# A two-layer decoder trunk with a top-2-of-8 expert layer on one core: expert 0 with 64 slots in place of 96, three experts gathered together, and the slots' places copied across partitions

## The chip, the cores and the metric

The kernel runs on one core of one Trainium2 chip. The metric is the device time of one execution in microseconds (us). Durations come from one profiled execution of the kernel before.

## The reference

Two residual layers over 256 tokens of 1024 channels, all in float32. Each layer is a mixer (projections, sparse and dilated attention, gates) and a feed-forward part; the first layer's is dense, the second's is a choice of two experts out of eight for each token. Only that last part is touched by the change:

```python
def moe_swiglu(h, router, w1, w3, w2):
    B, S, D = h.shape
    x = h.reshape(B * S, D)
    logits = (x @ router).astype(F32)
    top_v, top_i = lax.top_k(logits, TOP_K)
    wts = jax.nn.softmax(top_v, axis=-1)
    combine = jnp.sum(jax.nn.one_hot(top_i, N_EXPERTS, dtype=F32) * wts[..., None], axis=1)
    out = jnp.zeros((B * S, D), F32)
    for e in range(N_EXPERTS):
        out = out + combine[:, e:e + 1] * swiglu(x, w1[e], w3[e], w2[e]).astype(F32)
    return out.reshape(B, S, D).astype(h.dtype)
```

`w1` and `w3` of an expert are 1024 x 2816, `w2` is 2816 x 1024: 34.6 MB for one expert, 276.8 MB for the eight. After it come a residual add and a final RMSNorm.

## The kernel before, in words

The program runs the first layer (mixer, dense feed-forward), the second layer's mixer, and then the function `moe`. Its stages follow one another on TensorE (PE). Every instruction goes through a helper that records it at one line, L137, so rows are told apart by their tiles.

**Routing and slots.** `moe` ranks the eight logits of each token, and numbers the tokens of each expert: token number n of an expert gets slot n. Experts are taken in an order that depends on how many tokens they have. `PLACE` says which rank stands at which place of the order: rank 0 is always expert 0 (its weights are asked for before the routing is known), and ranks 1 to 7 are the others by falling count. `BLOCKS` says how many blocks of 32 slots the expert at each place has. If some expert has more tokens than slots, `tc.If(ms["over"] > 0)` runs a further pass over all eight experts for the rest. What follows calls an expert by its place, 0 to 7.

**picks and gather.** `picks` makes on VectorE (DVE) a selection matrix `Pm` (token by slot, one where the token has that slot) for a group of `GROUPS`. `gather` multiplies the tokens (`kh`, `kl`, high and low part of each) by it on PE and so brings the group's tokens as columns into the tile `xge`: 8 channel blocks x 2 token halves x 2 parts = 32 matmuls for a group, each as wide as the group's columns. The first gather stands ahead of expert 0; the one of a later group stands inside the last product of the expert before it (`k0 == 12`).

**One expert** of `nb` blocks: `wide_layer` for `w1` and for `w3` (columns up to 2048, 8 weight tiles each), the remaining 768 columns of both (8 tiles, `rest`), then `w2` (11 tiles of two k blocks). A block's 32 slots are the stationary operand, in one of four column strips of 32 of the array. For every weight tile PE goes over the blocks, so an expert with three blocks takes about half as long again on PE as one with two. Behind the second `rest` tile, `places` brings `Pm` into the form `PT` (slot by token), and the transposes `turned` bring the gated activations from `sg` into the tile `He`, which is read by the `w2` products. The scatter (`prev`) multiplies the result by `PT` and adds it to the residual `x`; it stands at the third weight tile of the following expert.

**places before.** `PT` has three variants. They differ in partitions 96 to 127: where an expert has three blocks, the fourth column strip of `w2` holds sums of another block for each third of the columns. For each token half, `places` transposes `Pm` on PE, makes for three blocks two more products of 32 columns with the identity that land on partitions 96 to 127, and copies with ACT and DVE.

**Weights.** 17 tiles of 1 MB hold weights (`rawx`, `raw`, and pairs `whi`, `wlo`). `weight()` issues a load from the SyncE queue (SP) in the order in which the weights are used; a load waits until PE has read the tile that it replaces. The first 17 are issued during the second layer's mixer. For the last expert `w2` is loaded in two column halves, and behind the third tile of the first half the same queue loads the final norm's gain into the tile `xge` (`load_gain`, L310), which must wait until PE has read `xge` for the last time, in the last expert's `rest` products. Every weight load behind it in the queue waits with it.

Of the kernel before, what the change touches and what calls it, by code (L numbers as in the profile page):

```python
# [9 lines left out]
F32 = mybir.dt.float32  # L10
F32R = mybir.dt.float32r
I32 = mybir.dt.int32
AF = mybir.ActivationFunctionType
OP = mybir.AluOpType
AX = mybir.AxisListType

SEQ, D, DEPTH = 256, 1024, 2
HD, ROT = 64, 16
HALF = ROT // 2
NT = SEQ // 128  # L20
DB = D // 128
# [16 lines left out]
SC = HD ** -0.5  # L38


PLACE = 0, 5, 1, 6, 2, 3, 4, 7
BLOCKS = 3, 2, 3, 2, 3, 3, 3, 2

GROUPS = (0,), (1, 2), (3, 4), (5, 6), (7,)

CHUNKS = {2: ((0, 512), (512, 512)), 3: ((0, 352), (352, 336), (688, 336))}
FA = 2048
# [52 lines left out]
def f(ap):  # L100
    return ap.bitcast(F32)
# [3 lines left out]
def tile_hybrid(ctx: ExitStack, tc: tile.TileContext, x, positions, norm_mix, w_in, pos_k, pos_v,  # L105
# [12 lines left out]
    def bank(tag, dt=F32):  # L118
        return psum.tile([128, 512], dt, name="ps_" + tag, tag=tag)
# [26 lines left out]
    V, S, T = Queue("V", nc.vector), Queue("S", nc.scalar), Queue("T", nc.tensor)  # L146

    def mm(o, l, r, start, stop):
        return T.matmul(o, l, r, start=start, stop=stop, skip_group_check=True)

    def tr(o, i, idt):
        return T.transpose(o, i, idt)
# [19 lines left out]
    ident = ct[:, C_ID:C_ID + 128]  # L172
# [273 lines left out]
    def copy(eng, o, i):  # L446
        if eng == "S":
            S.activation(o, i, AF.Copy)
        else:
            V.tensor_copy(o, i)  # L450
# [520 lines left out]
    ms = {}  # L971
# [121 lines left out]
    def moe():  # L1093

        mp, L, kh, kl = ms["mp"], ms["L"], ms["kh"], ms["kl"]
# [22 lines left out]
        rx = mp.tile([128, NT], F32, name="rx")  # L1118
# [10 lines left out]
        slots = ct[:, C_SLOT:C_SLOT + 128]  # L1129
# [37 lines left out]

        def picks(g, sl, blocks):

            Pm = ms["pm"].tile([128, 2, NT, 128], F32R, name="Pm", bufs=2)  # L1170
            for i, r in enumerate(g):
                n = 32 * blocks[r]
                for t in range(NT):
                    for c in range(0, 128, n):
                        m = min(n, 128 - c)
                        V.tensor_tensor(Pm[:, i, t, c:c + m], slots[:, :m], sl[:, t, r:r + 1].to_broadcast([128, m]),
                                        op=OP.is_equal)
            return Pm

        def experts(ep, blocks, bases, Pm=None):  # L1180
            first = bases is None
            if first:
                sl = sls
            else:
                sl = ep.tile([128, NT, NE], F32, name="slot2", bufs=1)
# [2 lines left out]

            def gather(g, Pm, by_tile=False):

                n = 32 * max(blocks[r] for r in g)
                ng = len(g)
                xg = ep.tile([128, DB, 192], F32, name="xge", bufs=1)
                pts = [bank("mm") for _ in range(DB // 2)]
                for ts in ((t,) for t in range(NT)) if by_tile else (range(NT),):
                    for d in range(DB):
                        o = pts[d // 2][:, d % 2 * 256:d % 2 * 256 + ng * n]
                        cs = slice(d * 128, (d + 1) * 128)
                        for t in ts:
                            mm(o, kh[:, t, cs], Pm[:, :ng, t, :n], t == 0 and d % 2 == 0, False)  # L1200
                            mm(o, kl[:, t, cs], Pm[:, :ng, t, :n], False, t == NT - 1)
                for d in range(0, DB, 2):
                    copy("SV"[d // 2 % 2], xg[:, d:d + 2, :ng * n],
                         pts[d // 2].rearrange("p (k c) -> p k c", k=2)[:, :, :ng * n])
                return xg, n

            def scales(Pm):

                rg = ep.tile([128, 16], F32, name="rg", bufs=1)
                pr = bank("a")  # L1210
                for s in range(blocks[0]):
                    for t in range(NT):
                        for c in range(4):
                            mm(pr[32 * c:32 * c + 32, s:s + 1], f(Pm)[:, 0, t, 32 * s:32 * s + 32], rx[:, t:t + 1],
                               t == 0 and s == 0, t == NT - 1)
                V.tensor_copy(rg[:, :blocks[0]], pr[:, :blocks[0]])
                return rg
# [19 lines left out]
            fin = None  # L1237
# [18 lines left out]
                    ms["index"][r] = nc.values_load(ints[0:1, r:r + 1], engines=(mybir.EngineType.SP,),  # L1256
                                                    min_val=0, max_val=NE - 1)

            group = {g[0]: g for g in GROUPS}
            Pms, rg = {}, None  # L1260
            Pms[0] = Pm = Pm or picks(GROUPS[0], sl, blocks)
            in_order("VST" if first else "T")
            xg, wide = gather(GROUPS[0], Pm, by_tile=True)
            if first:
                rg = scales(Pm)
                weights()
# [4 lines left out]
            for r in range(NE):  # L1271
                nb = blocks[r]
                if r in group:
                    g = group[r]
                if r + 1 in group:
                    Pms[r + 1] = picks(group[r + 1], sl, blocks)
                i = g.index(r)
                Pm = Pms[g[0]]
                sc = [rg[:, s:s + 1] if first and r == 0 else None for s in range(nb)]
                He = ep.tile([128, FB, 96], F32, name="He", bufs=1)  # L1280
                xs = [slice(i * wide + 32 * s, i * wide + 32 * s + 32) for s in range(nb)]


                def wide_layer(tag):
# [30 lines left out]
                for k in range(DB):  # L1315
# [5 lines left out]
                    if k == 1:  # L1321
                        PT = places(ep, Pm, i, nb)
# [50 lines left out]
                for half in range(2) if by_half else (None,):  # L1373
                    for k0 in range(0, FB, 4):
                        ks = range(k0, min(k0 + 4, FB))
                        ws = {}
                        if by_half:
                            hs = weight()
                            ws = {k: hs[(k - k0) // 2][:, (k - k0) % 2 * 512:(k - k0) % 2 * 512 + 512] for k in ks}
                        else:  # L1380
                            for k in ks[::2]:
                                ws[k], ws[k + 1] = weight()
                        lanes = [[] for _ in range(4)]
                        for k in ks:
                            for n in range(len(ch)) if half is None else (half,):
                                for s in range(nb):
                                    if nb == 2:
                                        q = k % 2 * 2 + s
                                    else:
                                        q = 3 if s == n and k % 4 != 3 and k < FB - 1 else s  # L1390
                                    lanes[q].append((n, k, s))
                        for j in range(max(len(l_) for l_ in lanes)):
                            for q, l_ in enumerate(lanes):
                                if j < len(l_):
                                    n, k, s = l_[j]
                                    c0, cw = ch[n]
                                    mm(Y[n][32 * q:32 * q + 32, :cw], He[:, k, 32 * s:32 * s + 32],
                                       ws[k] if by_half else ws[k][:, c0:c0 + cw], (q, n) not in marks, k >= FB - 2)
                                    marks.add((q, n))
                        if k0 == 0 and not half:  # L1400
                            for p in range((nb + 1) // 2):
                                turned_rest(p)
                        if k0 == 8 and last and not half:
                            fin = ep.tile([128, DB, 192], F32, name="xge", bufs=1).rearrange("p d c -> p (d c)")
                            load_gain(fin[:, :D], final_norm)
                        if k0 == 12 and r + 1 in group:
                            xg, wide = gather(group[r + 1], Pms[r + 1])
                        if k0 == 4 and half == 1:
                            in_order("VST")
                            final(0)  # L1410
# [17 lines left out]
        def places(ep, Pm, i, nb):  # L1428

            PT = ep.tile([128, 3, SEQ], F32R, name="PT", bufs=1)  # L1430
            pts = [bank(("mm", "a")[t]) for t in range(NT)]
            for t, pt in enumerate(pts):
                tr(pt[:, :128], f(Pm)[:, i, t, :128], ident)
                if nb == 3:
                    for n in (1, 2):
                        mm(pt[96:, n * 128:(n + 1) * 128], f(Pm)[:, i, t, 32 * n:32 * n + 32], ident, True, True)
            for t, pt in enumerate(pts):
                ts = slice(t * 128, (t + 1) * 128)
                S.activation(PT[:, 0, ts], pt[:, :128], AF.Copy)
                if nb == 3:  # L1440
                    V.tensor_copy(PT[:96, 1:, ts], pt[:96, None, :128].to_broadcast([96, 2, 128]))
                    V.tensor_copy(PT[96:, 1:, ts], pt[96:, 128:384].rearrange("p (n c) -> p n c", n=2))
            return PT

        def finish(ep, fin):
# [23 lines left out]
        ms["rk"] = mp  # L1469
        Pm0 = picks(GROUPS[0], slot, BLOCKS)  # L1470
        rstd(rx)
# [67 lines left out]
```

## Time and profile before

| | |
|---|---|
| median of 3 runs | 1320.09 us (1318.83 to 1321.11) |
| the profiled execution's own time | 1320.82 us |
| its span, first to last instruction | 1318.9 us |
| PE busy | 1286.2 us, 98% |
| PE weight loads busy | 855.1 us, 65% |
| DVE busy | 546.9 us, 41% |
| ACT busy | 411.8 us, 31% |
| moved by DMA | 383.32 MB |

How to read it: a busy PE need not be a PE at its peak, since matmuls overlap, and a share over the whole span says nothing about one stage. The experts run from about 631 us to the end. In a row of instructions the first number is the start in us from the span's start, the second the length of the merged run; from the start of one row to the start of the next is what the work of the row costs in time. A float32 matmul shows as two instructions.

### The profile page before, as it was taken

The page shows a single profiled execution, that of the slowest core. Times are in us where ns is not written, and L with a number is a line of the kernel's source. Part 1 is how long each engine was busy: PE and PEld are TensorE (multiplying, and loading weights), DVE is VectorE, ACT ScalarE, POOL GpSimd, SP SyncE. Part 2 cuts the span into 40 slices and gives each one's busy share as a digit, 9 for nine tenths or more (in the row PEclk, how much of TensorE's full clock was granted, in tenths as well). Part 3 has the DMA queues.
Part 4 walks back from the last instruction along what each step waited for, and adds up shares of the span by engine and source line. Part 5 has one row for each costly group of instructions (what it writes and reads, how often), then busy time and mean ns, then how long its engine had stood idle before and what let it go on. Part 6 is the DMA issues. An engine that isn't in the chain of part 4 may idle for free. (4 is left out here: it accounts for less than half of the span.)

```text
span 1318.9 us, 26882 instructions
## 1 busy us (share of the span) xinstructions
PE 1286.2 (98%) x11256; PEld 855.1 (65%) x11256; DVE 546.9 (41%) x1259; ACT 411.8 (31%) x756; POOL 0.2 (0%) x4
## 2 busy tenths in 40 slices
PE   7999999999999999999999999999999999999994
PEld 6888998999888888998337333473335635536431
DVE  6788668666548787676311110201101101110112
ACT  6676546544436576553201010100001001010001
POOL 0000000000000000000000000000000000000000
PEclk9999999999999999998899999999999999999897
DMA  8744435555556654469699999999999999999854
GB/s 289 254 133 124 141 116 192 192 192 192 192 177 200 223 160 118 140 229 417 207 382 399 375 423 419 419 423 418 423 417 414 424 411 422 417 411 424 318 211 190
DMA packets 122945, 383.32 MB, mean 291 GB/s; under 512 B 10720, under 2 KB 17216, under 8 KB 110400
## 3 DMA queue, kind: packets, MB, share of 16 engines
q1 hardware_dynamic: 122816, 381.53, 76.4%
q8 instruction: 90, 1.47, 0.4%
q14 instruction: 39, 0.32, 0.1%
HBM read 380.45 MB, written 1.05 MB: 289 GB/s over the span
## 5 line engine op out<-in xcount | busy, mean ns | idle before, releaser
L137 DVE TENSOR_TENSOR wlo<-raw,whi 128x1024 fp32r<-128x1024 f32 (+1 forms) x186 | 221.8, 1201 | 111.8 <-ACT whi L137 110.7
L137 ACT ACTIVATE whi<-raw 128x1024 fp32r<-128x1024 f32 (+1 forms) x186 | 191.3, 1040 | 160.1 <-PE ps_mm L137 106.0
L137 PE MATMUL ps_mm<-rawx,xge 128*32 128x384 f32 (+1 forms) x1912 | 189.5, 543 | 0.0
L137 PEld LDWEIGHTS ps_mm<-rawx,xge 128*32 128x32 f32 x1912 | 67.9, 111 | 108.8 <-issue 101.4
L137 PE MATMUL ps_mm<-whi,hTh 128*128 128x512 f32 (+2 forms) x320 | 121.2, 379 | 2.4 <-ACT whi L137 2.4
L137 PE MATMUL ps_mm<-hTh,whi 128*128 128x256 f32 x432 | 122.6, 284 | 0.0
L137 PE MATMUL ps_mm<-hTh,wlo 128*128 128x256 f32 x432 | 120.4, 279 | 0.0
L137 PE MATMUL ps_mm<-hTl,whi 128*128 128x256 f32 x432 | 120.4, 279 | 0.0
L137 PE MATMUL ps_mm<-wlo,hTh 128*128 128x512 f32 (+2 forms) x320 | 119.6, 374 | 0.4 <-DVE wlo L137 0.4
L137 PE MATMUL ps_mm<-whi,hTl 128*128 128x512 f32 (+2 forms) x320 | 119.3, 373 | 0.0
L137 PE MATMUL ps_a<-rawx,He 128*32 128x336 f32 (+2 forms) x1104 | 96.4, 493 | 5.6 <-DMA rawx<-in_moe_w_dram 5.6
L137 DVE TENSOR_TENSOR sg<-ps_a,sg 128x512 f32<-128x512 f32 x18 | 12.4, 691 | 186.1 <-PE ps_a L137 186.1
L137 PEld LDWEIGHTS ps_mm<-hTh,whi 128*128 128x128 f32 x432 | 81.7, 189 | 1.7 <-issue 1.0
L137 PEld LDWEIGHTS ps_a<-rawx,He 128*32 128x32 f32 x1104 | 54.6, 112 | 42.9 <-issue 18.0
L137 PEld LDWEIGHTS ps_mm<-hTh,wlo 128*128 128x128 f32 x432 | 81.6, 189 | 0.2
L137 PEld LDWEIGHTS ps_mm<-hTl,whi 128*128 128x128 f32 x432 | 81.6, 189 | 0.0
L137 PEld LDWEIGHTS ps_mm<-whi,hTh 128*128 128x128 f32 x320 | 60.5, 189 | 13.3 <-ACT whi L137 2.7
L137 PE MATMUL ps_mm<-raw,xge 128*32 128x512 f32 (+1 forms) x680 | 67.8, 546 | 0.0
L137 PEld LDWEIGHTS ps_mm<-wlo,hTh 128*128 128x128 f32 x320 | 60.5, 189 | 11.1 <-DVE wlo L137 1.0
L137 PE MATMUL ps_a<-whi,He 128*32 128x336 f32 (+2 forms) x448 | 67.2, 479 | 0.0
L137 PEld LDWEIGHTS ps_mm<-whi,hTl 128*128 128x128 f32 x320 | 60.5, 189 | 9.9
L137 PE MATMUL ps_a<-whi,xge 128*32 128x512 f32 x296 | 64.9, 592 | 0.0
(306 smaller groups left out, 1967.0 us busy)
## 6 DMA issues: line engine op xcount, KB each, us to landing
rawx<-in_moe_w_dram SPq DMA_DIRECT2D x103, 1024.0 KB, 12.4
raw<-in_moe_w_dram SPq DMA_DIRECT2D x50, 1024.0 KB, 12.1
raw<-in_w_in_dram SPq DMA_DIRECT2D x42, 1024.0 KB, 5.1
rawx<-in_moe_w_dram SPq DMA_DIRECT2D x96, 384.0 KB, 7.5
raw<-in_ffn_w_dram SPq DMA_DIRECT2D x33, 1024.0 KB, 5.0
whi<-in_moe_w_dram SPq DMA_DIRECT2D x62, 512.0 KB, 11.2
wlo<-in_moe_w_dram SPq DMA_DIRECT2D x62, 512.0 KB, 10.8
raw<-in_moe_w_dram SPq DMA_DIRECT2D x28, 384.0 KB, 7.6
```

The source lines that it names most:

```text
L137: return lambda *a, **k: queue(self.e, getattr(self.eng, name)(*a, **k))
```

## The change

Three things change. Expert 0 has two blocks (64 slots) in place of three, and the order becomes `PLACE = 0, 1, 2, 5, 3, 6, 4, 7`, so that experts with two and three blocks alternate more. `Pm` is packed without gaps: the columns of the group's experts stand one behind the other, and three experts (96 + 96 + 64, and 96 + 64 + 96 columns) share one gather of 256 columns, so there are four gathers in place of five. And `places` transposes only the expert's own slots, into one PSUM bank for both token halves, and the rows for partitions 96 to 127 (with two blocks 64 to 127) are copied by ACT from lower partitions.

```diff
-PLACE = 0, 5, 1, 6, 2, 3, 4, 7
-BLOCKS = 3, 2, 3, 2, 3, 3, 3, 2
-
-GROUPS = (0,), (1, 2), (3, 4), (5, 6), (7,)
+PLACE = 0, 1, 2, 5, 3, 6, 4, 7
+BLOCKS = 2, 3, 3, 2, 3, 2, 3, 2
+
+GROUPS = (0,), (1, 2, 3), (4, 5, 6), (7,)
+GROUPS3 = (0,), (1, 2), (3, 4), (5, 6), (7,)
...
-                n = 32 * max(blocks[r] for r in g)
-                ng = len(g)
-                xg = ep.tile([128, DB, 192], F32, name="xge", bufs=1)
+                n = 32 * sum(blocks[r] for r in g)
+                xg = ep.tile([128, DB, 256], F32, name="xge", bufs=1)
...
-                            mm(o, kh[:, t, cs], Pm[:, :ng, t, :n], t == 0 and d % 2 == 0, False)
-                            mm(o, kl[:, t, cs], Pm[:, :ng, t, :n], False, t == NT - 1)
+                            mm(o, kh[:, t, cs], Pm[:, t, :n], t == 0 and d % 2 == 0, False)
+                            mm(o, kl[:, t, cs], Pm[:, t, :n], False, t == NT - 1)
...
             PT = ep.tile([128, 3, SEQ], F32R, name="PT", bufs=1)
-            pts = [bank(("mm", "a")[t]) for t in range(NT)]
-            for t, pt in enumerate(pts):
-                tr(pt[:, :128], f(Pm)[:, i, t, :128], ident)
-                if nb == 3:
-                    for n in (1, 2):
-                        mm(pt[96:, n * 128:(n + 1) * 128], f(Pm)[:, i, t, 32 * n:32 * n + 32], ident, True, True)
-            for t, pt in enumerate(pts):
-                ts = slice(t * 128, (t + 1) * 128)
-                S.activation(PT[:, 0, ts], pt[:, :128], AF.Copy)
-                if nb == 3:
-                    V.tensor_copy(PT[:96, 1:, ts], pt[:96, None, :128].to_broadcast([96, 2, 128]))
-                    V.tensor_copy(PT[96:, 1:, ts], pt[96:, 128:384].rearrange("p (n c) -> p n c", n=2))
+            pt = bank("a")
+            n = 32 * nb
+            for t in range(NT):
+                tr(pt[:n, t * 128:(t + 1) * 128], f(Pm)[:, t, i:i + n], ident)
+            if nb == 3:
+                for c in range(3):
+                    S.activation(PT[96:, c], pt[32 * c:32 * c + 32, :SEQ], AF.Copy)
+                V.tensor_copy(PT[:96], pt[:96, None, :SEQ].to_broadcast([96, 3, SEQ]))
+            else:
+                S.activation(PT[64:, 0], pt[:64, :SEQ], AF.Copy)
+                V.tensor_copy(PT[:64, 0], pt[:64, :SEQ])
             return PT
```

`GROUPS3` is for the further passes. The order of the instructions stays as it was on every engine up to the first `picks`, and the SP queue's rows are the same throughout.

PE in `rest` of an expert with three blocks, from the second `rest` tile to the first `w2` product; before (expert 0):

```order
L137 MATMUL ps_mm<-rawx,xge 32x384 x12
L137 MATMUL ps_mm<-ct,Pm 128x128
L137 MATMUL ps_mm<-ct,Pm 32x128 x2
L137 MATMUL ps_a<-ct,Pm 128x128
L137 MATMUL ps_a<-ct,Pm 32x128 x2
L137 MATMUL ps_a<-ct,sg 128x128 x12
L137 MATMUL ps_mm<-rawx,xge 32x384 x72
```

and with the change (expert 1, where lines have moved by one):

```order
L138 MATMUL ps_mm<-rawx,xge 32x384 x24
L138 MATMUL ps_a<-ct,Pm 96x128 x2
L138 MATMUL ps_a<-ct,sg 128x128 x12
L138 MATMUL ps_mm<-rawx,xge 32x384 x72
```

`ct` holds the identity, `Pm` the selection, `sg` the gated activations. The four products of 32 columns are gone and the two transposes are narrower; nothing else moves there.

ACT at the same place of an expert with three blocks, from the `silu` of the wide layer to the copies behind `w2`; before (expert 2):

```order
L137 ACTIVATE sg<-ps_mm 128x512 x3
L137 ACTIVATE PT<-ps_mm 128x128
L137 ACTIVATE PT<-ps_a 128x128
L137 ACTIVATE He<-ps_a 128x4x2x32 x3
L137 ACTIVATE sb<-ps_mm 64x384 x3
```

and with the change (expert 1):

```order
L138 ACTIVATE sg<-ps_mm 128x512 x3
L138 ACTIVATE PT<-ps_a 32x256 x3
L138 ACTIVATE He<-ps_a 128x4x2x32 x3
L138 ACTIVATE sb<-ps_mm 64x384 x3
```

Three copies in place of two stand ahead of the copies into `He`. On DVE one copy of 96 partitions x 768 elements stands there in place of four of 256 elements.

## Rows read from the trace of the kernel before

**Rows 1.** The page's first part: busy us, share of the span, instructions.

```profile
PE 1286.2 (98%) x11256; PEld 855.1 (65%) x11256; DVE 546.9 (41%) x1259; ACT 411.8 (31%) x756; POOL 0.2 (0%) x4
```

**Rows 2.** Windows: busy us (instructions) of each engine; granted clock, DMA share, GB/s.

```profile
735.00:1218.00 483.00, 482.96 (x5112) 219.19 (x5112) 61.68 (x128) 38.34 (x87) 0.00 (x0) 1.00 1.02 418
1218.00:1234.00 16.00, 16.00 (x154) 10.95 (x157) 2.09 (x5) 1.92 (x5) 0.00 (x0) 0.79 0.73 279
1260.00:1276.00 16.00, 16.00 (x179) 6.27 (x172) 3.32 (x6) 2.19 (x6) 0.00 (x0) 1.00 0.08 29
1279.00:1302.00 23.00, 17.24 (x144) 4.34 (x136) 2.10 (x3) 2.14 (x6) 0.00 (x0) 1.00 0.89 346
...
1140.00:1170.00 30.00, 30.00 (x270) 10.05 (x266) 2.98 (x6) 1.79 (x3) 0.00 (x0) 1.00 1.02 406
```

**Rows 3.** Waits from 560 us (PE: 1279 to 1304): us, times, longest.

```profile
SPq L998 <- PE ps_mm L137: 38.7, 20, 16.2
SPq L310 <- PE ps_mm L137: 20.9, 1, 20.9
...
PE ps_a L137 <- DMA rawx<-in_moe_w_dram: 5.6, 6, 1.5
```

**Rows 4.** Timeline of SP's issues: the first reload and the gain's load.

```profile
636.38 16.53 SPq L998 DMA_DIRECT2D rawx<-in_moe_w_dram  x14
...
1274.34 0.35 SPq L310 DMA_DIRECT2D xge<-in_final_norm_dram  x1
```

**Rows 5.** Timeline of PE: first products of experts 0, 1, 2, 5, 6 and 7.

```profile
630.97 1.94 PE L137 MATMUL ps_mm<-rawx,xge 128*32 128x512 f32 x8
...
726.84 0.62 PE L137 MATMUL ps_mm<-rawx,xge 128*32 128x512 f32 x1
...
788.44 0.61 PE L137 MATMUL ps_mm<-rawx,xge 128*32 128x512 f32 x4
...
1040.67 0.62 PE L137 MATMUL ps_mm<-rawx,xge 128*32 128x512 f32 x1
...
1132.75 0.79 PE L137 MATMUL ps_mm<-rawx,xge 128*32 128x512 f32 x2
...
1231.95 0.62 PE L137 MATMUL ps_mm<-rawx,xge 128*32 128x512 f32 x1
```

**Rows 6.** Timeline of PE: `places` of experts 0 (three blocks) and 1 (two).

```profile
679.01 0.88 PE L137 MATMUL ps_mm<-ct,Pm 128*128 128x128 f32 x5
679.82 0.88 PE L137 MATMUL ps_a<-ct,Pm 128*128 128x128 f32 x5
680.63 1.53 PE L137 MATMUL ps_a<-ct,sg 128*128 128x128 f32 x12
682.10 11.82 PE L137 MATMUL ps_mm<-rawx,xge 128*32 128x384 f32 x144
693.73 5.37 PE L137 MATMUL ps_a<-rawx,He 128*32 128x336 f32 x72
...
759.94 0.33 PE L137 MATMUL ps_mm<-ct,Pm 128*128 128x128 f32 x1
...
760.21 1.04 PE L137 MATMUL ps_a<-ct,sg 128*128 128x128 f32 x8
```

**Rows 7.** Timeline of PE: pieces of gathers and of a scatter.

```profile
629.15 0.41 PE L137 MATMUL ps_mm<-Pm,kh 128*128 128x96 f32 x1
629.36 0.41 PE L137 MATMUL ps_mm<-Pm,kl 128*128 128x96 f32 x1
...
715.54 0.36 PE L137 MATMUL ps_mm<-Pm,kh 128*128 128x192 f32 x1
...
719.29 0.75 PE L137 MATMUL ps_a<-whi,He 128*32 128x336 f32 x5
...
733.38 0.32 PE L137 MATMUL ps_a<-yh,PT 128*128 128x336 f32 x1
733.54 0.32 PE L137 MATMUL ps_a<-yl,PT 128*128 128x336 f32 x1
```

More of the change, by code (lines that the diff above doesn't have):

```diff
@@ L1168, in picks @@
         def picks(g, sl, blocks):
-            Pm = ms["pm"].tile([128, 2, NT, 128], F32R, name="Pm", bufs=2)
-            for i, r in enumerate(g):
+            Pm = ms["pm"].tile([128, NT, 256], F32R, name="Pm", bufs=2)
+            c = 0
+            for r in g:
                 n = 32 * blocks[r]
                 for t in range(NT):
[L1174 to L1177, printed above, removed]
+                    V.tensor_tensor(Pm[:, t, c:c + n], slots[:, :n], sl[:, t, r:r + 1].to_broadcast([128, n]),
+                                    op=OP.is_equal)
+                c += n
             return Pm
@@ L1196, in gather @@
                     for d in range(DB):
-                        o = pts[d // 2][:, d % 2 * 256:d % 2 * 256 + ng * n]
+                        o = pts[d // 2][:, d % 2 * 256:d % 2 * 256 + n]
                         cs = slice(d * 128, (d + 1) * 128)
                         for t in ts:
-                            mm(o, kh[:, t, cs], Pm[:, :ng, t, :n], t == 0 and d % 2 == 0, False)
-                            mm(o, kl[:, t, cs], Pm[:, :ng, t, :n], False, t == NT - 1)
+                            mm(o, kh[:, t, cs], Pm[:, t, :n], t == 0 and d % 2 == 0, False)
+                            mm(o, kl[:, t, cs], Pm[:, t, :n], False, t == NT - 1)
                 for d in range(0, DB, 2):
-                    copy("SV"[d // 2 % 2], xg[:, d:d + 2, :ng * n],
-                         pts[d // 2].rearrange("p (k c) -> p k c", k=2)[:, :, :ng * n])
-                return xg, n
+                    copy("SV"[d // 2 % 2], xg[:, d:d + 2, :n],
+                         pts[d // 2].rearrange("p (k c) -> p k c", k=2)[:, :, :n])
+                return xg
             def scales(Pm):
@@ L1213, in scales @@
                         for c in range(4):
-                            mm(pr[32 * c:32 * c + 32, s:s + 1], f(Pm)[:, 0, t, 32 * s:32 * s + 32], rx[:, t:t + 1],
+                            mm(pr[32 * c:32 * c + 32, s:s + 1], f(Pm)[:, t, 32 * s:32 * s + 32], rx[:, t:t + 1],
                                t == 0 and s == 0, t == NT - 1)
@@ L1257, in load_index @@
                                                     min_val=0, max_val=NE - 1)
-            group = {g[0]: g for g in GROUPS}
+            parts = GROUPS if first else GROUPS3
+            group = {g[0]: g for g in parts}
             Pms, rg = {}, None
-            Pms[0] = Pm = Pm or picks(GROUPS[0], sl, blocks)
+            Pms[0] = Pm = Pm or picks(parts[0], sl, blocks)
             in_order("VST" if first else "T")
-            xg, wide = gather(GROUPS[0], Pm, by_tile=True)
+            xg = gather(parts[0], Pm, by_tile=True)
             if first:
@@ L1276, in experts @@
                     Pms[r + 1] = picks(group[r + 1], sl, blocks)
-                i = g.index(r)
+                i = 32 * sum(blocks[q_] for q_ in g[:g.index(r)])
                 Pm = Pms[g[0]]
@@ L1280, in experts @@
                 He = ep.tile([128, FB, 96], F32, name="He", bufs=1)
-                xs = [slice(i * wide + 32 * s, i * wide + 32 * s + 32) for s in range(nb)]
+                xs = [slice(i + 32 * s, i + 32 * s + 32) for s in range(nb)]
                 def wide_layer(tag):
@@ L1403, in experts @@
                         if k0 == 8 and last and not half:
-                            fin = ep.tile([128, DB, 192], F32, name="xge", bufs=1).rearrange("p d c -> p (d c)")
+                            fin = ep.tile([128, DB, 256], F32, name="xge", bufs=1).rearrange("p d c -> p (d c)")
                             load_gain(fin[:, :D], final_norm)
                         if k0 == 12 and r + 1 in group:
-                            xg, wide = gather(group[r + 1], Pms[r + 1])
+                            xg = gather(group[r + 1], Pms[r + 1])
                         if k0 == 4 and half == 1:
```

## The prediction

> **What bounds the kernel now.** I read four views in this order. The page's first part shows PE busy for 98% of the span and DVE and ACT for less than half [rows 1]. The windows then separate the stages: from 735 to 1218 us, inside the expert stage, PE is busy all the time at a granted clock of 1.00, and the DMA engines move 418 GB/s at a share of 1.02, so both are full at once [rows 2]. The waits say which of the two has slack. In the whole expert stage PE waits for weights 5.6 us in six pieces, all of them behind 1279 us, while SP, which issues the loads, waits for PE: 38.7 us at the loads of the remaining columns, and once 20.9 us at L310, the load of the final gain [rows 3]. So PE is the bound, and the transfers run up against it: 17 full tiles are on the chip when expert 0 begins at 630.97 us [rows 5], and the next load leaves at 636.38 us, when PE has read the first tile [rows 4].
>
> The windows show two of the holes this leaves: 279 GB/s from 1218 to 1234 us, and 29 GB/s from 1260 to 1276 us [rows 2]. The second is the one that the end hangs on. L310 can leave only when PE has finished the last `rest` product, at 1274.34 us [rows 4], and the last 8 MB of weights stand behind it in SP's queue. From there on the end is transfer time and a tail: PE waits for weights in 1279 to 1302 us, then come the last scatter, the norm and the output. So whatever PE saves before that last `rest` product moves L310 and the end by the same amount, until the transfers alone set the pace.
>
> **The change, part by part, on PE.**
>
> *One block less for expert 0.* Expert 5 has three blocks and no gather in it: 1040.67 to 1132.75 is 92.1 us. Expert 1 has two and none: 726.84 to 788.44 is 61.6 us [rows 5]. Both contain the scatter of a three-block predecessor. The difference, 30.5 us, is what expert 0 loses. The low clock at its beginning stays either way. The 1.35 us by which `places` is cheaper with two blocks is inside.
>
> *Places of the four experts that keep three blocks.* Before, ten instructions take 679.01 to 680.63, 1.62 us; the two transposes of a two-block expert take 759.94 to 760.21, 0.27 us [rows 6]. The changed code leaves two transposes with fewer columns, a form that the trace does not have. Ends: nothing, or 0.65 us, each transpose counted as two of the old instructions of 0.16 us. I take 0.27 us, the nearest row. Gain 4 x 1.35 = 5.4 us (3.9 to 6.5).
>
> *The copies behind them* I cost at nothing on PE. The cover is the rest of the `rest` products: from 682.10 to the first `w2` product at 693.73 us, 11.6 us in which ACT and DVE must copy `PT` and then `He` [rows 6]. ACT and DVE are busy 31% and 41% of the span [rows 1]. If a copy across partitions cost so much that the cover ran out, PE would wait at `w2` for the excess, once for each expert. `PT` itself is needed only by the scatter in the next expert.
>
> *Gathers.* Three of 192 columns go, at 715.54 to 719.29 = 3.75 us each, 11.25 us [rows 7]. Two of 256 columns come, which no row shows. Ends: as long as the old one, 3.75 us, or in proportion to the columns, 5.0 us. The nearest row is the scatter, a stream of the same kind of operands: 336 columns take 0.16 us from start to start [rows 7], which makes 0.122 us for 256, and 32 of them 3.9 us. I take 2 x 3.9 = 7.8 us. Gain 3.4 us (1.2 to 3.8). The Trainium skill ("TensorE: Matmul & The Clock Gate", section "Back-to-back issue gap") gives columns divided by 2.4 GHz and 2.5 ns on top; by it the two gathers would take 7.0 us and the forecast would be 0.8 us lower. Its value for 336 columns, 0.143 us, is below the measured 0.16 us, so I stay with the row.
>
> *First gather, 64 columns for 96.* It runs at the low clock with 0.21 us from start to start for 96 columns, while 192 columns at the full clock take 3.75 / 32 = 0.117 us [rows 7]: about half the time for twice the columns at twice the clock. So the columns do not set its length. I take 0 (0 to 2.2 us, a third of 32 x 0.21).
>
> Picks, scales and the first copies shrink by fractions of a microsecond. SP's rows do not change, and no wait is added to any queue.
>
> **Sum on PE:** 30.5 + 5.4 + 3.4 = 39.3 us (35.6 to 43.0).
>
> **Do the transfers allow it?** 276.8 MB less the 17.6 MB already there and 0.5 MB for the gain are 259.7 MB, at 418 GB/s 621 us [rows 2]. Before, they take from 636.38 us [rows 4] to about 1274.3 + 8.9 MB / 418 GB/s = 1296 us, 659 us; so 38 us of holes can go. With two blocks the first tile is read in two thirds of the 5.4 us, and the first load leaves 1.8 us earlier. That allows some 40 us, hardly more than PE gives. Stepping both along, with 90.7 us for a three-block expert and 61.6 or 65.5 us for a two-block one, PE comes to expert 6 at about 1096 us, its first tile at 1092 to 1094 us, and to the last `rest` product some 6 us behind its tile. PE stays just ahead of being starved. I take 1 us off for places where they do touch: 38.3 us. The profiled execution took 1320.8 us, 0.7 us above the median of the runs; 1320.8 - 38.3 = **1282.5 us**. Its own range, from the bounds of the sum, is 1278 to 1287 us.
>
> **The rivals.**
>
> *The transfers become the bound.* For it: the margin is a few microseconds, and there are stretches of 30 us at 406 GB/s [rows 2]. Against it: 418 over 483 us is a mean that holds these. At 410 GB/s, between the two, 259.7 MB take 633 us, 12 us more, and the limit of 40 us becomes 28 us: 1293 us. At 414 it is 1287 us. I give 1287 to 1296 us.
>
> *The clock falls more often.* In 1218 to 1234 us the granted clock is 0.79 [rows 2], that is 6.7 us at 1.2 GHz in place of 2.4, and 3.4 us of PE time lost. It fell inside the gather of 64 columns, and that gather remains. If PE, now nearer to its data, also lost the clock while waiting in expert 5 and in expert 7, two such stretches would give 1282.5 + 6.7 = 1289 us. Against it: between 1279 and 1302 us PE waits six times, 5.6 us in all [rows 3], at a clock of 1.00 [rows 2]. The Trainium skill ("TensorE: Matmul & The Clock Gate", section "HAM oscillation — how this bites in real kernels") says that waits for data between short bursts send the clock back; by that, this rival holds. The trace does not show it for waits of this size.
>
> *Slower: the further pass runs.* Expert 0 now has 64 slots, and 512 assignments over eight experts are 64 on average. One token too many, and all experts run again with three blocks: at least 276.8 MB / 418 GB/s = 662 us more, about 1945 us. It is decided at 65 tokens for expert 0, or 65 for one at ranks 5 to 7, or 97 elsewhere. Worked out from the reference on its drawn inputs, the experts get 53, 79, 65, 94, 45, 50, 71 and 55 tokens: expert 0 fits, ranks 1 to 4 (94, 79, 71, 65) fit 96, the others (55, 50, 45) fit 64. So it is nearly excluded.
>
> *No change: the copies hold PE up.* Were each of ACT's three copies of 32 partitions to take some 7 us, `w2` of four experts would start about 10 us late (3 x 7.2 - 11.6 us of cover [rows 6]), and the gain would be gone: about 1320 us. Nothing speaks for such a price.
>
> **How the numbers follow.** Forecast 0.66; transfers as the bound 0.16; clock 0.08; still faster, below 1278 us (the upper bounds of the sum together with faster transfers), 0.05; further pass 0.02; copies 0.03, of which a third comes out slower. The range 1277 to 1292 us holds the forecast, the clock and most of the transfer rival, and leaves out about 0.15. A measurement of this kernel can tell about 0.2%, 2.6 us, from no change: faster 0.95, same 0.02, slower 0.03.
>
> **What would show it.** In the profile of the changed kernel: expert 0 takes about 65 us on PE in place of 95.9; `places` of three blocks takes 0.3 us; gathers of 256 columns take 3.9 us; L310 leaves at about 1236 us, and its wait is a few microseconds in place of 20.9; the DMA engines show 418 GB/s from 640 to 1255 us with no hole. The forecast is wrong if PE waits for weights by more than some 3 us ahead of the last `rest` product (then the transfers are the bound), if the granted clock falls in further stretches, or if L310 still waits 15 us or more.

## The result and the profile after

| | before | changed |
|---|---|---|
| median of the runs beside each other | 1319.46 us (4 runs, 1316.17 to 1321.11) | 1287.68 us (4 runs, 1283.72 to 1290.28) |
| the profiled execution's own time | 1320.82 us | 1283.72 us |
| its span | 1318.9 us | 1281.8 us |

The ratio of the medians is 0.9758, 95% interval 0.9739 to 0.9778: 31.8 us faster. The time lies inside the range. It is 5.2 us above the forecast of 1282.5 us, and the saving is 31.8 us where the sum gave 38.3.

The page's first part, the row that answers to [rows 1]:

```profile
PE 1245.5 (97%) x10745; PEld 820.4 (64%) x10745; DVE 539.0 (42%) x1223; ACT 410.2 (32%) x749; POOL 0.2 (0%) x4
```

PE is 40.7 us less busy and does 511 matmuls less. So PE lost about what the sum says it would (39.3 us); the time fell by less. The windows of the changed kernel, columns as in [rows 2], tell where the rest is:

```profile
634.00:640.00 6.00, 6.00 (x63) 1.67 (x58) 3.94 (x12) 1.86 (x3) 0.00 (x0) 1.00 0.96 329
...
634.00:1096.00 462.00, 458.63 (x4787) 198.95 (x4783) 62.35 (x123) 42.19 (x89) 0.00 (x0) 1.00 1.02 416
...
640.00:1220.00 580.00, 576.10 (x6008) 254.18 (x6003) 73.65 (x139) 50.54 (x109) 0.00 (x0) 1.00 1.02 418
1220.00:1240.00 20.00, 18.91 (x205) 6.93 (x197) 4.09 (x8) 2.45 (x6) 0.00 (x0) 1.00 1.03 404
1240.00:1262.00 22.00, 18.33 (x128) 4.33 (x124) 2.10 (x3) 2.04 (x5) 0.00 (x0) 0.84 0.98 379
```

The two holes of [rows 2] are gone. The DMA engines now run at a share near 1.0 from 634 us to 1262 us, and PE, which was busy 482.96 of 483 us, stands still for 3.9 us in 580. The waits of the whole span (us in total, times, longest), PE's and then SP's:

```profile
PE ps_a L138 <- DMA rawx<-in_moe_w_dram: 7.2, 9, 3.0
...
PE ps_a L138 <- DMA whi<-in_moe_w_dram: 1.1, 2, 0.9
...
PE ps_mm L138 <- DMA rawx<-in_moe_w_dram: 0.5, 1, 0.5
...
SPq L999 <- PE ps_mm L138: 19.2, 13, 11.8
...
SPq L311 <- PE ps_mm L138: 3.2, 1, 3.2
```

Against [rows 3]: SP waits for PE 19.2 us at the remaining columns in place of 38.7, and 3.2 us at the gain's load in place of 20.9. PE waits for weights 3.9 us already ahead of expert 6, where before no such wait stood ahead of 1279 us. SP's issues, which answer to [rows 4]:

```profile
632.51 9.77 SPq L999 DMA_DIRECT2D rawx<-in_moe_w_dram  x11
...
1234.95 0.35 SPq L311 DMA_DIRECT2D xge<-in_final_norm_dram  x1
1235.51 18.50 SPq L1012 DMA_DIRECT2D rawx<-in_moe_w_dram  x9
```

And PE's timeline (start, us; idle time ahead and its releaser in brackets), against [rows 5 to 7]: the first products of experts 0, 1, 2, 5, 6 and 7, a gather of 256 columns (its first and last of 32), `places` of a three-block expert, three `w2` tiles of expert 5, and two of the last expert:

```profile
628.81 16.51 PE L138 MATMUL ps_mm<-rawx,xge 128*32 128x512 f32 x128
...
685.00 0.38 PE L138 MATMUL ps_mm<-Pm,kh 128*128 128x256 f32 x1
...
688.62 0.28 PE L138 MATMUL ps_mm<-Pm,kl 128*128 128x256 f32 x1
...
694.00 7.91 PE L138 MATMUL ps_mm<-rawx,xge 128*32 128x512 f32 x72
...
741.36 0.42 PE L138 MATMUL ps_a<-ct,Pm 128*96 128x128 f32 x2
741.62 1.47 PE L138 MATMUL ps_a<-ct,sg 128*128 128x128 f32 x12
...
783.88 0.79 PE L138 MATMUL ps_mm<-rawx,xge 128*32 128x512 f32 x2
...
1029.96 0.79 PE L138 MATMUL ps_mm<-rawx,xge 128*32 128x512 f32 x2
...
1082.31 1.92 PE L138 MATMUL ps_a<-rawx,He 128*32 128x512 f32 x16 [0.56 <-DMA rawx<-in_moe_w_dram]
1084.79 1.92 PE L138 MATMUL ps_a<-rawx,He 128*32 128x512 f32 x16 [0.55 <-DMA rawx<-in_moe_w_dram]
1087.28 1.92 PE L138 MATMUL ps_a<-rawx,He 128*32 128x512 f32 x16 [0.56 <-DMA rawx<-in_moe_w_dram]
...
1097.19 7.93 PE L138 MATMUL ps_mm<-rawx,xge 128*32 128x512 f32 x72 [0.53 <-DMA rawx<-in_moe_w_dram]
...
1192.60 0.62 PE L138 MATMUL ps_mm<-rawx,xge 128*32 128x512 f32 x1
...
1245.94 4.50 PE L138 MATMUL ps_a<-rawx,He 128*32 128x512 f32 x20 [3.01 <-DMA rawx<-in_moe_w_dram]
...
1262.61 2.78 PE L138 MATMUL ps_a<-rawx,He 128*32 128x512 f32 x24 [0.61 <-DMA rawx<-in_moe_w_dram]
```

Expert 0 takes 65.2 us. In expert 5 a `w2` tile of 1.05 MB starts every 2.48 us, which is 423 GB/s, though PE needs only 1.7 us for it where it does not wait (in the kernel with less bytes, below): PE is fed at the pace of the transfers there. The brackets understate it. They show 0.5 to 0.7 us for each tile, 3.9 us in all, while expert 5 takes 67.2 us where the same work without waits takes 61.6 (below).

### The profile page after: what moved, and what is told of

Same layout as the page of the kernel before. It is cut to its first block, busy times and chain, and to the rows that moved or that the text cites. A ratio compares the mean times of both kernels' runs of the same rounds, so it can differ in the third digit from the quotient of the medians.

```text
span 1281.8 us, 25825 instructions
## 1 busy us (share of the span) xinstructions
PE 1245.5 (97%) x10745; PEld 820.4 (64%) x10745; DVE 539.0 (42%) x1223; ACT 410.2 (32%) x749; POOL 0.2 (0%) x4
## 3 DMA queue, kind: packets, MB, share of 16 engines
HBM read 380.45 MB, written 1.05 MB: 298 GB/s over the span
## 5 line engine op out<-in xcount | busy, mean ns | idle before, releaser
L138 PE MATMUL ps_mm<-rawx,xge 128*32 128x384 f32 (+1 forms) x1848 | 182.6, 543 | 0.5 <-DMA rawx<-in_moe_w_dram 0.5
L138 PEld LDWEIGHTS ps_mm<-rawx,xge 128*32 128x32 f32 x1848 | 64.1, 111 | 107.3 <-issue 95.8
L138 PEld LDWEIGHTS ps_a<-rawx,He 128*32 128x32 f32 x984 | 45.8, 113 | 50.0 <-issue 22.9
L138 DVE TENSOR_TENSOR yl<-ps_a,yh 128x512 fp32r<-128x512 f32 (+2 forms) x20 | 11.6, 585 | 129.9 <-ACT yh L138 129.5
L138 PE MATMUL ps_a<-whi,He 128*32 128x336 f32 (+2 forms) x408 | 64.4, 493 | 1.1 <-DMA whi<-in_moe_w_dram 1.1
L138 PE MATMUL ps_mm<-raw,xge 128*32 128x512 f32 (+1 forms) x624 | 62.5, 546 | 0.0
```

Of the source, the lines that this page charges most:

```text
L138: return lambda *a, **k: queue(self.e, getattr(self.eng, name)(*a, **k))
```

## The experiments

Executions of one kernel differ by up to 13 us, but in its traces the experts hardly differ: from expert 0's first product (e0) to the end of the span the changed kernel takes 652.9, 652.3 and 652.5 us in three traces, while e0 itself lies between 628.8 and 636.0 us over all traces. So parts are compared by this stretch, and medians stand beside it. "Last `rest`" is where the last `rest` product ends, which releases L310/L311; 0 to 6 are the times from an expert's first product to the next one's. The table is worked out from the PE timelines and SP's issues of each trace.

| kernel | 0 | 1 | 2 | 3 | 4 | 5 | 6 | e0 to last `rest` | e0 to end |
|---|---|---|---|---|---|---|---|---|---|
| before | 95.9 | 61.6 | 95.2 | 61.8 | 95.2 | 92.1 | 99.2 | 643.2 | 688.0 |
| before, again | 94.8 | 61.6 | 95.2 | 61.8 | 95.2 | 92.1 | 95.9 | 638.8 | 683.8 |
| changed | 65.2 | 89.9 | 90.6 | 65.6 | 89.9 | 67.2 | 95.4 | 606.1 | 652.9 |
| changed, second and third | 64.3, 63.9 | 89.9 | 90.6 | 65.6 | 89.9 | 67.6 | 94.2, 93.7 | 605.3, 604.8 | 652.3, 652.5 |
| blocks only | 64.9 | 91.3 | 96.0 | 61.6 | 95.2 | 61.7 | 98.5 | 611.5 | 656.4 |
| places only | 93.2 | 61.6 | 93.8 | 62.6 | 93.8 | 90.6 | 94.5 | 632.3 | 676.7 |
| places and gathers | 94.1 | 61.6 | 89.9 | 67.4 | 89.9 | 94.5 | 90.6 | 630.2 | 674.2 |
| old order | 64.7 | 70.5 | 89.9 | 77.1 | 89.9 | 94.5 | 90.6 | 619.6 | 664.4 |
| late gain | 64.4 | 89.9 | 90.6 | 65.7 | 89.9 | 67.5 | 93.7 | 605.0 | 651.7 |
| less bytes | 64.2 | 89.9 | 90.6 | 65.6 | 89.9 | 61.6 | 93.7 | 597.8 | 642.3 |
| less PE | 64.9 | 89.0 | 90.3 | 65.2 | 89.0 | 70.1 | 94.5 | 605.4 | 652.1 |
| less of both | 64.2 | 89.0 | 90.3 | 65.3 | 89.0 | 61.3 | 92.8 | 593.7 | 636.9 |

Two theories stand against each other. By the first PE still sets the end, and every term of the sum pays in full. By the second the transfers have become the bound, and what PE saves beyond that point comes back as waits.

**The changed kernel again**, twice, the first beside *blocks only*, *places and gathers* and *old order*, the second beside *late gain*, *less bytes* and *less PE*; *before, again*, *places only* and *less of both* ran beside one another. The median of before was 1319.28, 1315.86 and 1315.78 us in these three sets, so ratios compare across sets and medians only within one. No edit.

> The changed kernel once more, beside its parts on one chip, to see how far its executions spread and whether a slower one shows where. Theory A (TensorE's work up to the last rest product sets the end, the transfers keep just ahead): 1283 us as in the first profile, spread no larger than that of the kernel before (5 us). Theory B (the transfers set the end, PE has run out of slack): 1284 to 1291 us, spread larger, and the slower executions show a lower GB/s between 650 and 1230 us and more PE waits for weights, not a lower clock.

> The changed kernel beside its variants on one chip, in more rounds. Both theories: 1283 to 1293 us as in the eight executions so far, median 1288.

Measured: 1288.01 us (4 runs, ratio 0.9779, 0.9749 to 0.9808) and 1285.6 us (ratio 0.9758, 0.9732 to 0.9784). From e0 the three traces agree within 0.6 us; expert 5 takes 67.6 us in both new ones. The runs spread over 9.3 us, as the second theory expected, but not for its reason: the second and the third trace (1283.57 and 1287.31 us) both move 418 GB/s from 640 to 1220 us, and 3.6 us of their difference lie ahead of e0.

**Before, again.** No edit.

> The kernel before once more, for a second trace. Its part from the first product of expert 0 to the end took 688.0 us in the first trace; in all traces of one changed version so far this part agrees within 0.6 us, while the program ahead of it differs by up to 7 us. Expected: 686 to 688.5 us for that part, with whatever start.

Measured: 1317.84 us, ratio 1.0003 (0.9977 to 1.0029), but 683.8 us from e0 where the first trace has 688.0, below the 686 to 688.5 expected. The window that answers to the second of [rows 2] starts a little earlier here, around the same gather:

```profile
1212.00:1228.00 16.00, 16.00 (x201) 12.04 (x196) 1.54 (x4) 1.86 (x5) 0.00 (x0) 1.00 0.96 385
```

No fall of the clock in the gather of 64 columns this time, and a shorter low stretch at expert 0 (94.8 in place of 95.9 us). The trace that the prediction worked from had both. Against this one the change saves 683.8 - 652.5 = 31.3 us, which agrees with the medians' 31.8; against the first trace it would be 35.1 to 35.7.

**Blocks only.** The new order and the two blocks for expert 0; `places` and gathers as before.

```diff
-PLACE = 0, 5, 1, 6, 2, 3, 4, 7
-BLOCKS = 3, 2, 3, 2, 3, 3, 3, 2
+PLACE = 0, 1, 2, 5, 3, 6, 4, 7
+BLOCKS = 2, 3, 3, 2, 3, 2, 3, 2
```

> Only the table changes: expert 0 with two blocks and the new order; gathers, Pm and places as before. Theory A: 30.5 us less than before, 1289.5 us, and so about 9 us slower than the whole change, since places (5.4 us) and gathers (3.4 us) are still to come. Theory B: the transfers' floor is reached by the block alone, so it is within 3 us of the whole change.

Measured: 1291.74 us (ratio 0.9797, 0.9775 to 0.9818). To the last `rest` product it saves 638.8 - 611.5 = 27.3 us against the second trace of before. But its clock fell at the 64-column gather (1186.84 to 1190.70 us), for 6.8 us at 1.2 GHz:

```profile
1186.00:1198.00 12.00, 12.00 (x106) 8.02 (x102) 0.58 (x2) 0.55 (x2) 0.00 (x0) 0.72 1.00 422
```

That is 3.4 us lost, so the block's term is 30.7 us, forecast 30.5. PE does not wait for weights ahead of the last expert: the transfers are not yet the bound. The other two parts save 8.8 us of PE by the sum, but only 656.4 - 652.5 = 3.9 us of time here (3.7 by the medians), and by this estimate 3.4 of these are the clock. The first theory asked for all 8.8; the second for no more than 3, which holds only without the clock's share.

**Places only.** The kernel before with the new `places`, on the old `Pm`.

```diff
-            pts = [bank(("mm", "a")[t]) for t in range(NT)]
...
+                tr(pt[:n, t * 128:(t + 1) * 128], f(Pm)[:, i, t, :n], ident)
...
+                    S.activation(PT[96:, c], pt[32 * c:32 * c + 32, :SEQ], AF.Copy)
```

> Only places changes: old blocks, old order, old gathers. Theory A and B alike (PE is far behind the transfers here): 5 x 1.35 = 6.8 us less from the first product of expert 0 to the end, 681 us, and a median some 7 us lower. Rival, that the copies across partitions hold PE up: less than 4 us, with PE waiting at the first w2 product for He.

Measured: 676.7 us from e0, 7.1 us less than the second trace of before; five three-block experts at the forecast 1.35 us are 6.8. The median, 1310.97 (ratio 0.995, 0.9925 to 0.9975), is lower by 4.8 us. Ahead of the last expert PE has one wait, of 0.5 us, and it is for weights: the copies from shifted partitions hold nothing up. The five three-block experts get 7.3 us shorter, and expert 3 gets 0.8 us longer, since that wait is in it. Both theories had PE far behind the transfers here; in expert 3 it was not.

**Places and gathers.** The changed kernel with the old blocks and order.

```diff
-PLACE = 0, 1, 2, 5, 3, 6, 4, 7
-BLOCKS = 2, 3, 3, 2, 3, 2, 3, 2
+PLACE = 0, 5, 1, 6, 2, 3, 4, 7
+BLOCKS = 3, 2, 3, 2, 3, 3, 3, 2
...
-GROUPS = (0,), (1, 2, 3), (4, 5, 6), (7,)
+GROUPS = (0,), (1, 2, 3), (4, 5), (6, 7)
```

> The opposite part: new places and packed gathers, but the old table of blocks and order; groups (0), (1,2,3), (4,5), (6,7), four gathers. Both theories, since PE is then far behind the transfers: places 5 x 1.35 = 6.8 us and one gather, 3.7 us, less; if the gather of 64 columns, which now is one of 160, no longer drops the clock, 3.4 us more. 10 to 14 us faster than before, 1306 to 1310 us. A rival that the copies across partitions hold PE up: less than 4 us faster.

Measured: 674.2 us from e0, 9.6 less than the second trace of before, of which the gathers are 9.6 - 7.1 = 2.5 us. The median over 10 runs, 1311.27 (ratio 0.9934, 0.9914 to 0.9954), gives 8.0 us. Both are less than the 10 to 14 expected. Here too PE meets the transfers in expert 3: it takes 67.4 us, with a wait of 0.6 us for a weight tile in it, where the changed kernel's two-block expert with a gather takes 65.6. Without these 1.8 us it would be some 11.4.

**Old order.** The changed kernel with two blocks for expert 0 and the order as before, so that the sequence of block counts is 2, 2, 3, 2, 3, 3, 3, 2.

```diff
-PLACE = 0, 1, 2, 5, 3, 6, 4, 7
-BLOCKS = 2, 3, 3, 2, 3, 2, 3, 2
+PLACE = 0, 5, 1, 6, 2, 3, 4, 7
+BLOCKS = 2, 2, 3, 2, 3, 3, 3, 2
...
-GROUPS = (0,), (1, 2, 3), (4, 5, 6), (7,)
+GROUPS = (0,), (1, 2, 3), (4, 5), (6, 7)
```

> The whole change but the order of the experts: blocks 2, 2, 3, 2, 3, 3, 3, 2, groups (0), (1,2,3), (4,5), (6,7). PE has the same work. Theory A in its plain form (the sum of PE's work decides): within 2 us of the whole change. Theory C (the order matters through the 17 weight tiles: two short experts first starve PE, three long ones in a row at the end leave it behind and bring back the hole at the load of the gain): 10 to 14 us slower than the whole change, PE waiting some 15 to 20 us for weights in experts 1 and 3, and the load of the gain leaving late, near 1247 us, with the DMA engines idle for some 10 us ahead of it.

Measured: 1298.69 us (ratio 0.9837, 0.9809 to 0.9864); 664.4 us from e0, 11.9 more than the changed kernel with as many blocks in all, as theory C has it. The groups follow the order; there are four gathers in both. Its windows, ahead of the gain's load, around expert 1 and around expert 3:

```profile
1240.00:1256.00 16.00, 16.00 (x179) 6.28 (x172) 3.73 (x7) 2.11 (x5) 0.00 (x0) 1.00 0.30 111
690.00:770.00 80.00, 74.36 (x673) 25.73 (x669) 10.18 (x17) 7.08 (x14) 0.00 (x0) 1.00 1.02 420
880.00:930.00 50.00, 44.97 (x387) 15.07 (x379) 4.57 (x12) 2.93 (x7) 0.00 (x0) 1.00 1.03 415
```

With three experts of two blocks among the first four, PE asks for weights faster than they come: experts 1 and 3 take 70.5 and 77.1 us, where such experts take 61.6 and 65.6 without waits, with the DMA engines full. Three experts of three blocks in a row leave the engines idle later, 111 GB/s. The 17 tiles cannot even this out. What the diff calls an order is worth over a third of the whole gain.

**Late gain.** The changed kernel; the load of the final gain stands behind the last weight load in SP's queue.

```diff
-                            load_gain(fin[:, :D], final_norm)
...
+                if last:
+                    load_gain(fin[:, :D], final_norm)
```

> The whole change, with the load of the final gain moved behind the last weight load, so that no weight load stands behind its wait for the last rest product. Theory A and B alike, if the hole at the gain's load still costs: PE's wait of 3 us at the first half of the last expert goes, with the transfer of 0.5 MB (1.3 us) out of the weights' way: 2 to 4 us less than the whole change. A rival: the tail is set by the rate alone and the gain now arrives late, at the output: no difference, or up to 2 us more.

Measured: 1284.06 us (ratio 0.9748, 0.9722 to 0.9774), 651.7 us from e0. That is 0.8 us less than the changed kernel, below the 2 to 4 us expected, and the intervals overlap: it is the lowest time of a complete kernel here, without being shown to be faster. So little hung on the gain's load any more, as the rival in the expectation had it.

**Less bytes, less PE, less of both.** Three kernels on the changed one. The first leaves out `w3`'s remaining 768 columns (25 MB, `w1`'s tile is used twice); the second leaves out the scatter's products with the low part `yl`; the third leaves out both.

```diff
-                for h, w in zip(hs, (moe1, moe3)):
+                for h, w in zip(hs[:1], (moe1, moe3)):
...
-                               hs[c // 2][:, c % 2 * (FR // 2):c % 2 * (FR // 2) + FR // 2], k == 0, k == DB - 1)
+                               hs[0][:, c % 2 * (FR // 2):c % 2 * (FR // 2) + FR // 2], k == 0, k == DB - 1)
...
-                    mm(o[:, :cw], l, yh[:, c0:c0 + cw], True, False)
-                    mm(o[:, :cw], l, yl[:, c0:c0 + cw], False, True)
+                    mm(o[:, :cw], l, yh[:, c0:c0 + cw], True, True)
```

> The whole change, but of the remaining 768 columns of w1 and w3 only w1's are loaded and used for both: 25 MB less to load, PE's work the same (the output then holds w1's columns in w3's place). Theory A: only the visible waits go, 5.6 us in expert 5 and 3 us at the last expert, 7 to 9 us less than the whole change's fastest executions, 1275 us; the spread stays, if it comes from elsewhere. Theory B: the transfers are the bound in most executions, so the median falls by more than the profile shows, 10 to 13 us, to 1275 to 1278 us, and the spread falls below 4 us.

> The opposite: PE's work less, bytes the same. The products with the low part of an expert's result are left out of the scatter, 42 matmuls of about 0.17 us, 7 us in all. Theory A: 5 to 7 us less than the whole change. Theory B: within 2 us of the whole change, and PE's waits for weights grow by what was saved.

> Both cuts in one: 25 MB less to load (w1's remaining columns used for w3's) and the low part of the expert's result left out of the scatter. The cut of PE's work alone gave 652.1 us from the first product of expert 0 to the end against 652.5 us, that of the bytes alone 642.3 us. Theory B (the transfers bind the whole change; without them PE binds again): the cut of PE's work now pays, 635 to 637.5 us. Theory A' (the scatter's products lie off PE's path in any case): 641.5 to 642.5 us.

Measured: 1279.43 us (ratio 0.9702, 0.9673 to 0.973), 1284.54 (0.9753, 0.9726 to 0.978) and 1271.63 (0.9671, 0.962 to 0.9722). From e0, with the changed kernel at 652.5 us:

| | all PE work | less PE work |
|---|---|---|
| all bytes | 652.5 | 652.1 |
| less bytes | 642.3 | 636.9 |

This settles which theory holds. PE work taken away alone is worth 0.4 us; expert 5 then waits longer (70.1 us). Bytes taken away alone are worth 10.2 us, and expert 5 falls to 61.6 us. Only with fewer bytes does the PE cut pay, 5.4 us. The medians point the same way with a wider margin: 1.1 us for PE work alone and 6.2 us for bytes alone, against 1285.6 us beside them; the 6.2 is less than the 10 to 13 us that the second theory expected. Taking the bytes away also takes 64 loads out of the queue; that the bytes count and not the number of loads is argued from the DMA share, 1.02 in the changed kernel and 0.98 in this one, and not tested apart. The window of the kernel with less bytes, where PE never stands still, and the waits for weights of the one with less PE work in 1060 to 1125 us:

```profile
640.00:1220.00 580.00, 580.00 (x6075) 256.15 (x6071) 78.78 (x158) 52.32 (x111) 0.00 (x0) 1.00 0.98 391
```

```profile
PE ps_a L138 <- DMA rawx<-in_moe_w_dram: 3.4, 6, 0.7
PE ps_a L138 <- DMA raw<-in_moe_w_dram: 1.0, 1, 1.0
```

The expectation of the second theory on the spread fell: with less bytes the runs still differ by 9 us (1271.74 to 1280.83), so the spread does not come from the experts' waits for weights.

## Why the prediction was right, and what it missed

*What bounds the kernel* held. L310 stood at the end of PE's work, and the change moved it, as L311, to 1234.95 us, forecast about 1236.

*The sum on PE* held. Where bytes do not bind, in the kernel with less bytes, the last `rest` product comes 638.8 - 597.8 = 41.0 us earlier than before, forecast 39.3 (35.6 to 43.0). By parts: the block 30.7 (forecast 30.5), with the clock put right by an estimate; `places` 7.3 for five experts (forecast 1.35 each), from two transposes that take 0.26 us (0.27); the copies nothing, since that kernel's PE does not wait ahead of the last expert; the gather of 256 columns 3.62 us from its first to its last start, 3.7 to 3.8 us in all (forecast 3.9), about the same as 192 columns. The bound "as long as the old one" was the right end. The estimate of 3.5 us by the Trainium skill ("TensorE: Matmul & The Clock Gate", section "Back-to-back issue gap") was not reached: 3.62 us over 31 gaps are 0.117 us from start to start. The prediction left out that the section gives this form for a matmul without the weight load beside it.

**The step that failed** is the 1 us taken off "for places where they do touch", a figure with no row behind it. The transfers take back 652.5 - 642.3 = 10.2 us: 6.0 in expert 5, about 1 in the last expert's loads ahead of its last `rest` product, about 3 behind it (47.6 us to the end in place of 44.5). The step rests on the prediction's line that 259.7 MB take 621 us at 418 GB/s. From the first reload at 632.51 us to the product that waited for its tile until 1262.61 us it takes 630 us, 412 GB/s. The 418 was right for the 580 us in between; but the first 6 us have 329 GB/s, and the last 42 us 404 and 379. The mean of the full stretch was used for its ends too. And the rate counts all queues, the bytes only one: what the queues of the changed kernel moved from 632 to 1262 us (packets, MB, share) holds 0.93 MB in the queues for instructions beside the 259.7 MB.

```profile
q1 hardware_dynamic: 65673, 259.74, 101.0%
q8 instruction: 50, 0.82, 0.5%
q14 instruction: 14, 0.11, 0.0%
```

By estimate the 8.8 us between 621 and 630 are 2.8 at the start (1.5 until 634 us, 1.3 in the 6 us behind it), 2.7 in the last 42 us, and 2.2 for the instructions at 415 GB/s; 1 us is left over. Counted from e0, PE without waits would have come to expert 6 after 462.8 us (forecast 1096 - 631 = 465), since three blocks take 89.9 us in place of 90.7; its first tile came after 468.4 us (forecast 461 to 463). So the margin of 2 to 4 us became 5.6 us of waiting. Of the 5.4 to 7.4 us by which that tile came late, the mean of 416 GB/s from 634 to 1096 us explains 2.2 us, the start before 634 us at most 1.5, and the instructions up to there at most 2.2; the rest is not told apart.

*The rivals.* The transfers as the bound is what happened, in mechanism: the condition named in the prediction, a PE that waits by more than 3 us ahead of the last `rest` product, is met. Its rate, 410 to 414 GB/s, holds the 412 worked out above. Of its times, 1287 to 1296 us, the median (1287.68) is just inside and the profiled execution (1283.72) below. The own range of the forecast, 1278 to 1287, held the profiled execution and missed the median by 0.7 us; its upper end is also 0.8 us above what the bounds of the sum give (1320.8 - 35.6 + 1 = 1286.2). So the wide range came true by way of the rival, and not by the sum that the forecast rests on. The copies were tested by *places only* and cost nothing; the further pass did not run.

*The clock.* In the changed kernel it fell twice between expert 0 and the last products: for 3.4 us right behind the 64-column gather of 1179.67 to 1183.43 us (0.83 over 1180 to 1190 us), and for 6.8 us from inside the wait of 3.01 us for the first `w2` tile behind the gain's load (0.84 over 1240 to 1262 us). The rule of the Trainium skill ("TensorE: Matmul & The Clock Gate", section "HAM oscillation — how this bites in real kernels"), that waits for data send the clock back, agrees with that second wait. It is not put to the test by the six waits of 0.5 to 0.7 us in expert 5, where the windows show 1.00: the section's waits are longer than the bursts between them, and here a burst is 1.92 us and the wait behind it 0.55. The fall cost next to nothing: the second trace of the changed kernel has neither fall and is only 0.6 us shorter from e0. Its last window:

```profile
1240.00:1262.00 22.00, 15.60 (x128) 3.97 (x129) 2.10 (x3) 2.04 (x5) 0.00 (x0) 1.00 0.97 375
```

PE is busy 2.7 us less there than in the first trace at nearly the same rate of transfers (375 and 379 GB/s): while these bind, a PE at the low clock only waits less.

*The base.* The trace of before carried 4.2 us that its other trace did not have. The sum did not count them as a gain, which was right for the medians. With 2.2 us ahead of e0 they are why the two profiled spans differ by 37.1 us and the medians by 31.8.

## What to carry to other kernels

Where two resources are full in the same stretch, the saving on one is only an upper bound: work out the other's time to the end with its rate at the start and the end too, not the mean of the full stretch alone, count all that its queues move, and take the later of the two as the forecast. The order of unequal pieces is then a term of its own, since a few buffers do not average a run of short pieces. Before differences of a few microseconds are explained, take a second trace of the kernel before and compare from a point inside the program.

## What the runs showed of the hardware that was not expected

In or right behind the last gather of 64 columns, with PE busy throughout and nothing waited for, the granted clock fell in some executions of one kernel and not in others: 6.8 us at 1.2 GHz in the first trace of before, none in the second, and a fall in 4 of the 11 traces with such a gather. In the two kernels whose last gather has 160 columns it did not fall. A single wait of 2.7 us for the first `w2` tile behind the gain's load went with a low stretch in the kernel with less PE work (0.84 over 1240 to 1262 us) and with none in the second and third trace of the changed one (1.00). What decides between the two is not shown.

In the traces the spread lies mostly ahead of the experts. In 5 of 13 traces the dense feed-forward of the first layer takes about 4.3 us longer, with the same instructions on a PE that is busy all the time at a granted clock of 1.00. The same window in the changed kernel and in the late-gain kernel:

```profile
310.00:338.00 28.00, 28.00 (x250) 28.00 (x249) 20.15 (x23) 13.80 (x17) 0.00 (x0) 1.00 0.61 196
```

```profile
310.00:338.00 28.00, 28.00 (x240) 28.00 (x239) 17.92 (x20) 12.48 (x15) 0.00 (x0) 1.00 0.55 185
```

250 matmuls in 28 us against 240. No run here tells what sets this pace; it stays open.
